# The last tokens in runs of 384 and 128 in place of 256 and 256, for the last down-projection and the final norm

## The chip, the cores and the metric

The kernel runs on one core of one Trainium2 chip, as one program. The metric is device time in microseconds (us) from launch to end, the median of several runs. A core has five engines that each work through a queue of their own: PE (TensorE, matrix products; its weight loads are listed apart as PEld), DVE (VectorE), ACT (ScalarE), POOL (GpSimd) and SP (SyncE, which here only issues transfers). They wait for each other through semaphores.

## The reference

A diffusion backbone of two layers works on 512 latent tokens (and, in the first layer, on 256 context tokens) of 1024 features. Each layer has a mixer (convolution, attention, gated linear attention) and a SwiGLU feed-forward of 2816 hidden features. The change concerns only the end of the second layer and what follows it, where the context tokens are no longer carried:

```python
x = x + gt2 * swiglu(rmsnorm(x, g2) * (1 + sc2) + sh2, w_up, w_down)   # last layer
return rmsnorm(x, final_norm_g)

def swiglu(h, w_up, w_down):
    a, b = jnp.split(h @ w_up, 2, axis=-1)
    return (jax.nn.silu(a) * b) @ w_down
def rmsnorm(x, g):
    return x * rsqrt(mean(x * x, -1) + 1e-6) * g
```

All inputs and the output (1, 512, 1024) are float32.

## The kernel before

**Layout.** The stream is held with features on the partitions: `xT[k]`, k from 0 to 7, is a tile of 128 features by 512 tokens. A run of tokens ("segment") is a triple (first, end, kind). `XS` is all 512 tokens; `XA` and `XB` are tokens 0 to 256 and 256 to 512. In the last layer `ga, gb = XA, XB`.

**Products.** For accuracy each float32 operand is split in two rounded parts (type float32r), hi and lo, and a product of matrices is three products on PE: hi by hi, hi by lo, lo by hi. ACT writes the hi part of a weight (a copy with rounding), DVE the lo part (a subtraction). `dense_pass(ws, X, segs, evict)` does one output block of 128 features for each segment: for every chunk of 128 input features three `S.mm`, each with weights of 128x128 and with as many columns as the segment has tokens, into a bank of PSUM of the kind "main" (three banks) and then `evict`. There are five banks of the kind "bank". All products are issued at line 139, all transposes at line 143; those are the lines of the helpers that the profile shows. Plain float32 products (not split) occur too, among them the sums over features with a column of ones.

**The hidden layer in blocks.** The 22 chunks of the hidden layer of the last layer come in blocks of 6, 6, 6 and 4 (`F_BLOCKS`). After each block its share of the down-projection is added to `xT` by `residual` (a DVE operation at line 199: PSUM times gate plus `xT`). The last block has 4 chunks. Its down-projection also has to deliver the squares for the final norm: `Sums.add` takes the square of the finished `xT[k]` on ACT (line 155) and adds it up on DVE (line 188), for each segment on its own.

**The tail.** `tail` does this last down-projection in an order of its own. Output blocks 0 and 1 were opened ahead (class `Opened`: their first three chunks fill PE while the last hidden chunk is being made), blocks 0, 1 and 2 are then done for both segments; blocks 3 to 7 are done for the first segment, their weights kept, the first segment's norm is handed on, and then blocks 3 to 7 are done for the second segment:

```python
for m in range(n_first, NK):                       # n_first = N_DOWN = 3
    ws.append((m, *w_next(keys[m]), 0))
    dense_pass(ws[-1:], X, (ga,), ev_)
norm_next(ga, sums[ga])
for j, w in enumerate(ws):
    dense_pass([w], X, (gb,), ev_)
    S.gave(plan[first + j]["b"])
S.gave(*drop)
norm_next(gb, sums[gb])
```

**The final norm.** `final_task(seg, sums)` is spawned for each segment. It becomes due `LAG_F` = 2100 ns (of the planner's time) after its spawning. It sums the squares over the partitions (one product with `ones` for each 128 tokens), takes the reciprocal root (`rstd`: DVE and ACT on a few columns), scales the eight `xT[k]` by the norm's weights in place (line 193: even k on DVE, odd k on POOL), and then for each 128 tokens transposes eight blocks back to tokens by features into two banks (line 143), scales them by the root (one half on DVE, line 193, one on ACT, line 181) and stores 512 KB from SP (line 2054).

**What sets the order.** The class `Plan` keeps a clock for each engine while the program is being written: an operation is booked at a cost (`COST`; for a rounded product `max(columns, 64) / 2.4` ns), and results are booked 150 ns (`HOP`) later. Tasks such as `final_task` are generators; `poll`, called after every chunk, steps those that are due by the planner's PE clock and for which there is room in the pools (`ROOM`: three main banks, five others). A bank counts as taken until the planned end of the operation that empties it. So the planner's costs decide between which products a task's instructions are put. Below it, the framework's scheduler may still move ready instructions of an engine ahead of others.

Of the kernel before, what the change touches and what calls it, by code (L numbers as in the profile page):

```python
# [20 lines left out]
SX = 512  # L21
# [21 lines left out]
CS = (SX, T, 1)  # L43
XA = (0, SX // 2, 0)
XB = (SX // 2, SX, 0)


C_ID, C_TL, C_TR, C_LV, C_BD, C_COS, C_SIN = 0, 128, 256, 384, 768, 896, 1408
# [271 lines left out]
def hybrid_kernel(ctx: ExitStack, tc: tile.TileContext, x, c, cx, c_ctx, w_mod, b_mod, norm1_g, norm2_g,  # L320
# [3 lines left out]
    S = Plan(tc)  # L324
# [16 lines left out]
    def tmp(rows=P, dt=F32):  # L341
        return S.took("t3", t3.tile([rows, T], dt, tag="t3", name="t3"))
# [83 lines left out]
    N_OUT2, N_DOWN = 1, 3  # L426
# [33 lines left out]
    for l in range(DEPTH):  # L460
# [19 lines left out]
        blocks = F_BLOCKS[l]  # L480
# [105 lines left out]
    def w_next(key):  # L586
        it = plan[at["use"]]
        assert it["key"] == key, (it["key"], key)
        if at["use"] and not plan[at["use"] - 1]["quarters"]:
            plan[at["use"] - 1]["read"] = True  # L590
        w_advance()
        at["use"] += 1
        if it["mod"]:
            S.last = max(S.last, it["t"])
        if it["quarters"]:
            return it
        return it["raw"] if it["mod"] else it["w"]
# [148 lines left out]
    def mod_steps():  # L746
        while at["use"] < len(plan) and plan[at["use"]]["mod"]:
            mod_step()
# [5 lines left out]
    def dense_pass(ws, X, segs, evict):  # L754

        n = len(X)
        for s in segs:
            t0, t1, _ = s
            S.room(main=len(ws))
            pts = [bank("main") for w in ws]  # L760
            for k in range(n):
                for (name, hi, lo, c0), pt in zip(ws, pts):
                    mm_ = 96 if name == "lr" else P
                    for a, b, st, sp in ((hi, 0, k == 0, False), (hi, 1, False, False), (lo, 0, False, k == n - 1)):
                        S.mm(pt[:mm_, :t1 - t0], a[:, k, c0:c0 + mm_], X[k][b][:, t0:t1], st, sp)
                S.poll()
            for w, pt in zip(ws, pts):
                evict(w[0], s, pt)
                S.gave(pt)
        S.poll()  # L770
# [497 lines left out]
    def split2(full, h, sl):  # L1268
        S.acopy(h[:, 0, sl], full)
        S.tt(h[:, 1, sl], full, h[:, 0, sl].bitcast(F32), ALU.subtract)  # L1270

    def residual(l, which, pt, m, s, sums=None):
        t0, t1, i = s
        S.stt(xT[m][:, t0:t1], pt[:, :t1 - t0], mod(l, which, m, i), xT[m][:, t0:t1], ALU.mult, ALU.add)
        if sums:
            sums[s].add(m)
# [454 lines left out]
    for l in range(DEPTH):  # L1731
        last = l == DEPTH - 1
        both = (XS, CS)
        sg = (XS,) if last else both
        ga, gb = (XA, XB) if last else (XS, CS)
        n = SX if last else T
# [191 lines left out]
        def tail(keys, X, which, n_first, norm_next, segs, drop, opened=()):  # L1928

            ga, gb = segs  # L1930
            sums = {s: Sums(s) for s in segs}
            ev_ = lambda m, s, pt: residual(l, which, pt, m, s, sums)
            for m in range(n_first):
                if m < len(opened):
                    opened[m].close(ev_)
                else:
                    dense_pass([(m, *w_next(keys[m]), 0)], X, segs, ev_)
                mod_steps()
            ws = []
            first = at["use"]  # L1940
            for m in range(n_first, NK):
# [8 lines that stand above are left out]
# [7 lines left out]
        blocks = F_BLOCKS[l]  # L1957
        units, made, opened = [], 0, []
        for bi, (f0, f1) in enumerate(blocks):
            ts_, tiles_ = [], []  # L1960

            def swiglu(sil, tt_):
                def ev_ab(name, s, pt):
                    t0, t1, _ = s
                    if name == "a":
                        S.act(sil[:, t0:t1], pt[:, :t1 - t0], AF.Silu)
                    else:
                        S.tt(sil[:, t0:t1], pt[:, :t1 - t0], sil[:, t0:t1], ALU.mult)
                        split2(sil[:, t0:t1], tt_, slice(t0, t1))
                tiles_.append(tt_)  # L1970
                ts_.append((tt_[:, 0], tt_[:, 1]))
                return ev_ab

            def begin(fs):

                units[:] = [Unit(l, f, norm) for f in fs]
                units[0].make("a11")
                units[0].make("s1")

            if bi == 0:  # L1980
                S.room(t3=2, act=2)
                sils = [tmp() for _ in range(2)]
                evs = [swiglu(sil, act_t(F32R)) for sil in sils]

                diff = []

                def hook0():
                    diff.append(S.spawn(norm.differences(("t1", "t2", "t3")), prio=-1,
                                        when=lambda: S.clk["pe"] if norm.done.get(gb, 0) == NK else None))
                Firsts((l, "up"), (ga, gb)).run(norm, lambda i, s, pt: evs[i % 2]("ab"[i // 2], s, pt),  # L1990
                                                (hook0, lambda: begin(range(2, f1))))
                S.gave(*sils)
                S.spawn(norm.differences(("t4",)), prio=-1, when=lambda: diff[0]["ready"] if diff[0]["done"] else None)
            heads = []

            def then():
                mod_steps()
                heads.append(w_next((l, "d", bi, 0)))
            run_units(units, 2, then)
            for u in units:  # L2000
                ts_.append(u.out)
                tiles_ += u.tiles

            ss = (ga, gb) if bi == len(blocks) - 1 else sg
            opened = [Opened((0, *heads[0], 0), ts_, ss)]
            opened.append(Opened((1, *w_next((l, "d", bi, 1)), 0), ts_, ss))
            if bi < len(blocks) - 1:
                ev_d = lambda m, s, pt: residual(l, 5, pt, m, s)
                for m in range(NK):
                    if m < len(opened):  # L2010
                        opened[m].close(ev_d)
                    else:
                        w = (m, *w_next((l, "d", bi, m)), 0)
                        if m == NK - 1:
                            begin(range(*blocks[bi + 1]))
                        dense_pass([w], ts_, sg, ev_d)
                    if m:
                        mod_steps()
                S.gave(*tiles_)
# [4 lines left out]
        keys = [(l, "d", len(blocks) - 1, m) for m in range(NK)]  # L2024
        if not last:
            norm = Normed(l + 1, V_N1, 1, 0)
            tail(keys, ts_, 5, N_DOWN, lambda s, sums: S.spawn(norm.task(s, sums), prio=-2), (ga, gb),
                 tiles_, opened)
        else:

            fin = []

            def final_task(seg, sums):
                t0, t1, _ = seg
                S.last += LAG_F
                yield dict(bank=1)
                pt = bank()
                nt = (t1 - t0) // P
                r = rstd(sums.total(pt), nt)
                S.gave(pt)  # L2040
                for k in range(NK):
                    S.ts(xT[k][:, t0:t1], xT[k][:, t0:t1], vec[:, V_FN + k:V_FN + k + 1], None, ALU.mult,
                         eng="pool" if k % 2 else "dve")
                for t in range(nt):
                    yield dict(bank=2)
                    pts = [bank(), bank()]
                    for k in range(NK):
                        S.tr(pts[k // 4][:, (k % 4) * P:(k % 4 + 1) * P], xT[k][:, t0 + t * P:t0 + (t + 1) * P], ident)
                    o = wp.tile([P, 1024], F32, tag="raw", name="raw", bufs=RAWS)
                    S.ts(o[:, :512], pts[0], r[:, t:t + 1], None, ALU.mult)  # L2050
                    S.amul(o[:, 512:], pts[1], r[:, t:t + 1])
                    S.gave(pts[0])
                    S.gave(pts[1])
                    nc.sync.dma_start(out[0, t0 + t * P:t0 + (t + 1) * P, :], o)
            tail(keys, ts_, 5, N_DOWN, lambda s, sums: fin.append(S.spawn(final_task(s, sums), prio=-2)), (ga, gb),
                 tiles_, opened)
            S.wait(*fin)

# [25 lines left out]
```

## Time and profile before

| what | us |
|---|---|
| median of the runs shown (three: 1618.64, 1619.19, 1624.01) | 1619.19 |
| the profiled execution, its own time | 1613.43 |
| its span, first to last instruction | 1611.6 |
| PE busy | 1569.9 (97% of the span) |
| DVE busy | 1219.3 (76%) |
| ACT busy | 757.0 (47%) |
| mean granted clock of PE | 0.997 of full speed |

The profiled execution is taken by the hardware profiler; times of instructions are counted from the span's start. A row of a group gives line, engine, operation, what it writes and reads by the program's names, shape and count, then busy time and mean duration of one. Products of a stream overlap, so their spacing is less than their duration. The chain of waits is followed back from the last instruction. The windows give busy time by engine for stretches of the span, with the count of instructions in brackets and the granted clock.

### The profile page before, as it was taken

How to read it: one execution, taken by the hardware profiler on the slowest of the kernel's cores; microseconds unless marked ns; L12 is line 12 of the kernel's file. 1: busy time of each engine (PE TensorE's matmuls, PEld its weight loads, DVE VectorE, ACT ScalarE, POOL GpSimd, SP SyncE). 2: the span in 40 equal slices, each digit the busy share in tenths (PEclk: the TensorE clock that was granted, in tenths of full speed). 3: DMA queues.
4: the chain of work that ended last, by engine and by line, in shares of the span. 5: the costliest groups of instructions: out<-in, count | busy, mean ns of one | idle time of the engine just before them, and what ended most of it. 6: DMA issues, size and time to landing. Idle time of an engine off the chain costs nothing.

```text
span 1611.6 us, 29142 instructions
## 1 busy us (share of the span) xinstructions
PE 1569.9 (97%) x11530; PEld 1387.9 (86%) x11530; DVE 1219.3 (76%) x2426; ACT 757.0 (47%) x1596; POOL 105.2 (7%) x122
## 2 busy tenths in 40 slices
PE   7999999999999999999999999998999999999998
PEld 5778777888888899999999988786889989989898
DVE  5687886668886788788888877879787956747576
ACT  4455544453663243242433546464474744536354
POOL 2000000000000000000000010000001112213012
PEclk9999999999999999999999999999999999999999
DMA  9831222253224544435334342211225466858552
GB/s 256 247 113 28 82 64 71 62 170 109 75 79 146 156 132 144 143 118 156 93 108 127 91 133 66 53 40 41 66 85 120 94 148 139 173 126 160 147 123 93
DMA packets 277578, 184.39 MB, mean 114 GB/s; under 512 B 30853, under 2 KB 258753, under 8 KB 277441
## 3 DMA queue, kind: packets, MB, share of 16 engines
q1 hardware_dynamic: 251008, 155.93, 33.7%
q0 software_dynamic: 24608, 21.27, 7.7%
q10 hardware_dynamic: 1824, 5.31, 0.9%
q8 instruction: 91, 1.49, 0.4%
q14 instruction: 47, 0.38, 0.1%
HBM read 175.14 MB, written 7.34 MB: 113 GB/s over the span
## 4 chain that ended last, share of the span: by engine, by line
PE 75%; DVE 10%; DMA 3%; ACT 3%; issue 2%; DVEq 0%; SPq 0%; ACTq 0%
PE main L139 49%; PE bank L139 24%; DVE act L188 3%; PE bank L143 3%; DMA raw<-in_w_mod_dram 2%; DVE t L188 1%; DVE wlo L188 1%; DMA raw<-in_w_up_dram 1%; ACT t L155 1%; DVE t L216 1%; DVE t L199 1%; DVE mx L207 1%; ACT t L177 1%; DVE t L193 0%; ACT whi L177 0%
## 5 line engine op out<-in xcount | busy, mean ns | idle before, releaser
L139 PE MATMUL main<-act,whi 128*128 128x512 f32 (+2 forms) x2772 | 667.8, 345 | 5.6 <-DVE act L199 2.1
L139 PEld LDWEIGHTS main<-act,whi 128*128 128x128 f32 x2772 | 460.5, 189 | 63.6 <-issue 12.1
L139 PE MATMUL main<-act,wlo 128*128 128x512 f32 (+2 forms) x1866 | 477.7, 334 | 3.0 <-DVE wlo L188 3.0
L139 PEld LDWEIGHTS main<-act,wlo 128*128 128x128 f32 x1866 | 315.1, 189 | 31.7 <-DVE wlo L188 5.2
L177 ACT CAST whi<-raw 128x512 fp32r<-128x512 f32 (+4 forms) x242 | 181.5, 751 | 292.6 <-PE main L139 201.0
L139 PE MATMUL bank<-act,whi 128*128 128x256 f32 (+2 forms) x1140 | 208.9, 309 | 1.1 <-DVE whi L188 0.7
L139 PEld LDWEIGHTS bank<-act,whi 128*128 128x128 f32 x1140 | 178.5, 190 | 8.1 <-DVE whi L188 1.0
L139 PE MATMUL bank<-act,wlo 128*128 128x256 f32 (+2 forms) x898 | 171.7, 308 | 2.2 <-DVE wlo L188 2.2
L199 DVE SCALAR_TENSOR_TENSOR act<-main,mods,act 128x256 f32<-128x256 f32 (+1 forms) x162 | 99.1, 615 | 78.1 <-PE main L139 76.6
L139 PEld LDWEIGHTS bank<-act,wlo 128*128 128x128 f32 x898 | 142.8, 190 | 6.3 <-DVE wlo L188 3.2
L188 DVE TENSOR_TENSOR wlo<-raw,whi 128x1024 fp32r<-128x1024 f32 (+4 forms) x122 | 122.6, 1005 | 20.7 <-ACT whi L177 19.9
L188 DVE TENSOR_TENSOR wlo<-raw,wlo 128x512 fp32r<-128x512 f32 x120 | 81.6, 686 | 39.4 <-ACT wlo L177 38.7
L199 DVE SCALAR_TENSOR_TENSOR t<-raw,cst,t 128x512 f32<-128x512 f32 x126 | 92.1, 745 | 20.4 <-DMA raw<-in_w_mod_dram 19.8
L188 DVE TENSOR_TENSOR whi<-raw,whi 128x512 fp32r<-128x512 f32 x120 | 81.3, 686 | 26.2 <-ACT whi L177 24.6
L155 ACT ACTIVATE t<-bank,nm 128x256 f32<-128x256 f32 (+1 forms) x144 | 69.8, 497 | 60.4 <-DVE nm L199 55.7
L177 ACT CAST wlo<-raw 128x512 fp32r<-128x512 f32 x120 | 74.6, 622 | 40.9 <-PE main L139 17.4
L177 ACT COPY t<-bank 128x512 f32<-128x512 f32 (+3 forms) x131 | 57.4, 453 | 72.1 <-PE bank L139 43.5
L139 PE MATMUL main<-act 128*128 128x256 f32 (+1 forms) x516 | 79.5, 309 | 0.0
L188 DVE TENSOR_TENSOR act<-t,act 128x512 fp32r<-128x512 f32 (+7 forms) x110 | 73.1, 681 | 7.0 <-ACT act L177 5.2
L155 ACT ACTIVATE t<-t 128x256 f32<-128x256 f32 (+3 forms) x108 | 58.1, 538 | 41.8 <-DVE t L188 41.3
L139 PE MATMUL main<-t,whi 128*128 128x512 f32 (+1 forms) x302 | 75.9, 338 | 0.0
L139 PEld LDWEIGHTS main<-act 128*128 128x128 f32 x516 | 70.9, 191 | 5.2 <-ACT t L155 0.4
(162 smaller groups left out, 2007.3 us busy)
## 6 DMA issues: line engine op xcount, KB each, us to landing
raw<-in_w_mod_dram SPq DMA_DIRECT2D x92, 512.0 KB, 4.3
raw<-in_w_up_dram SPq DMA_DIRECT2D x80, 512.0 KB, 4.6
raw<-in_w_in_dram SPq DMA_DIRECT2D x26, 512.0 KB, 3.9
t<-in_w_up_dram POOLq DMA_DIRECT2D x40, 256.0 KB, 5.2
raw<-in_w_down_dram SPq DMA_DIRECT2D x24, 384.0 KB, 3.9
raw<-in_w_down_dram SPq DMA_DIRECT2D x32, 256.0 KB, 2.8
raw<-in_w_down_dram SPq DMA_DIRECT2D x16, 320.0 KB, 3.4
raw<-in_w_up_dram POOLq DMA_DIRECT2D x20, 256.0 KB, 4.7
```

The lines of the kernel that those rows point to most:

```text
L139: self.pin("pe", self.nc.tensor.matmul(out, lhsT, rhs, start=start, stop=stop, **kw))
L143: self.pin("pe", self.nc.tensor.transpose(out, in_, ident))
L155: ins = self.pin("act", self.nc.scalar.activation(out, in_, func, **kw))
L177: self.pin("act", self.nc.scalar.copy(out, in_))
L188: self.pin(eng, self._v(eng).tensor_tensor(out, a, b, op))
L199: self.pin(eng, self._v(eng).scalar_tensor_tensor(out, a, s, b, op0, op1))
L207: self.pin("dve", self.nc.vector.tensor_reduce(out, in_, AX.X, op))
L216: self.pin("dve", self.nc.vector.copy_predicated(out, mask, data))
```

## The change

For the last block of the last layer the two segments are tokens 0 to 384 and 384 to 512. This goes for the openings of blocks 0 and 1, for the whole of `tail` there and so for the sums of squares and for both `final_task`s (three tiles of 128 tokens in the first, one in the second). The rest of the last layer, its other tail after the mixer included, keeps 256 and 256.

```diff
+XE, XF = (0, 384, 0), (384, SX, 0)
...
-            ss = (ga, gb) if bi == len(blocks) - 1 else sg
+            ends = (XE, XF) if last else (ga, gb)
+            ss = ends if bi == len(blocks) - 1 else sg
             opened = [Opened((0, *heads[0], 0), ts_, ss)]
             opened.append(Opened((1, *w_next((l, "d", bi, 1)), 0), ts_, ss))
...
-            tail(keys, ts_, 5, N_DOWN, lambda s, sums: fin.append(S.spawn(final_task(s, sums), prio=-2)), (ga, gb),
+            tail(keys, ts_, 5, N_DOWN, lambda s, sums: fin.append(S.spawn(final_task(s, sums), prio=-2)), ends,
                  tiles_, opened)
```

## The prediction

> **What bounds the kernel now.** I read the page first, then the chain of waits for the last 40 us, then the windows over the last stage, and last the timeline of PE for the price of one product of each width.
>
> ```profile
> span 1611.6 us, 29142 instructions
> PE 1569.9 (97%) x11530; PEld 1387.9 (86%) x11530; DVE 1219.3 (76%) x2426; ACT 757.0 (47%) x1596; POOL 105.2 (7%) x122
> PE 75%; DVE 10%; DMA 3%; ACT 3%; issue 2%; DVEq 0%; SPq 0%; ACTq 0%
> ```
>
> PE is busy for 97% of the span, so work added to it is paid in full unless it falls where PE waits. The change touches only the end, so that end is what has to be read (chain of waits, start, length, what):
>
> ```profile
> 1582.63 13.14 PE main L139 x108
> 1595.77 0.34 PE bank L139 x4
> 1596.11 2.98 PE main L139 x24
> 1599.09 0.87 PE bank L143 x8
> 1599.96 1.45 PE main L139 x12
> 1601.42 0.03 issue
> 1601.44 0.48 DVE act L199
> 1601.93 0.70 DVE raw L193
> 1602.63 0.34 DVE t L188
> 1602.97 0.14 issue
> 1603.11 0.59 PE bank L139 x4
> ...
> 1605.25 0.75 DVE raw L193
> 1606.00 0.66 DVEq L2080
> ```
>
> ```profile
> core 0: us, PE busy (x) PEld busy (x) DVE busy (x) ACT busy (x) POOL busy (x), PEclk, DMA share, GB/s
> 1576.30:1582.35 6.05, 6.05 (x51) 5.87 (x49) 3.68 (x7) 3.71 (x6) 0.00 (x0) 1.00 0.45 129
> 1582.35:1592.90 10.55, 10.55 (x89) 10.43 (x88) 10.09 (x26) 5.45 (x14) 5.45 (x4) 1.00 0.10 27
> 1592.90:1601.40 8.50, 8.50 (x74) 8.50 (x74) 6.26 (x20) 3.01 (x8) 3.47 (x3) 1.00 0.00 1
> 1601.40:1611.60 10.20, 3.26 (x29) 2.81 (x26) 3.74 (x10) 2.71 (x6) 1.20 (x1) 0.87 0.53 207
> ```
>
> Two regimes follow. Up to 1601.4 us, here called T, PE has no gap and its granted clock is 1.00: the last down-projection is bound by PE alone, and DVE (10.09 of 10.55 us in the first run's passes) is just covered. From T to the end there are 10.2 us of latency: residual, square, sum, root, scaling, store. The change makes the first regime dearer or not, and the second shorter or not.
>
> **The price of one product.** Before, every product of the stage has 256 columns. After, half have 384 and half 128. From rows of the timeline (start, length, xcount; the spacing is the length less the last one's own duration, over count less one):
>
> ```profile
> 1563.23 3.04 PE L139 MATMUL main<-act,whi 128*128 128x256 f32 x24
> ...
> 465.60 2.24 PE L139 MATMUL bank<-act,whi 128*128 128x384 f32 x12
> ...
> 1598.93 1.03 PE L143 MATMUL bank<-tab,act 128*128 128x128 f32 x8
> ...
> 1603.11 0.58 PE L139 MATMUL bank<-ones,t 128*128 128x1 f32 x4 [0.83 <-DVE t L188]
> ...
> 141.29 1.28 PE L139 MATMUL bank<-t,t 128*128 128x128 f32 x10
> ```
>
> ```profile
> L139 PE MATMUL main<-act,whi 128*128 128x256 f32 x1080 | 182.5, 286 | 1.4 <-ACT act L155 1.2 <-DVE act L199 0.2
> ...
> L139 PE MATMUL bank<-act,whi 128*128 128x384 f32 x360 | 68.0, 335 | 1.1 <-DVE whi L188 0.7 <-ACT whi L177 0.5
> ...
> L139 PE MATMUL bank<-t,t 128*128 128x128 f32 x80 | 10.4, 277 | 0.0
> ...
> L139 PE MATMUL bank<-ones,t 128*128 128x1 f32 x40 | 5.0, 235 | 0.8 <-DVE t L188 0.8
> ```
>
> ```profile
> L139 PEld LDWEIGHTS main<-act,whi 128*128 128x128 f32 x2772 | 460.5, 189 | 63.6 <-issue 12.1 <-ACT whi L177 3.9 <-ACT act L155 2.2
> ...
> L139 PEld LDWEIGHTS bank<-t,t 128*128 128x128 f32 x80 | 9.8, 191 | 0.6 <-issue 0.2 <-ACT t L177 0.2
> ```
>
> 256 columns: (3.04 - 0.29)/23 = 0.120 us. 384 columns: (2.24 - 0.335)/11 = 0.173 us. So 128 further columns cost 0.053 us, and by that line 128 columns alone would cost 0.067. Then 384 + 128 would equal 256 + 256 and the change would be free on PE. The short rows say that it is not: a product of a single column (ones) still takes (0.58 - 0.24)/3 = 0.11, eight transposes of 128 columns (1.03 - 0.27)/7 = 0.109, and ten plain float32 products of 128 columns (1.28 - 0.28)/9 = 0.112. Every product brings its own weight load, and the load of a rounded operand is as long as that of a plain one (189 and 191 ns), so I put the floor at 0.11.
>
> No row has a rounded (float32r) product of under 256 columns: all of them in this kernel are 256, 384 or 512 wide, and this is the unknown of the case. Bounds: 0.067 below (the line of streaming alone), and above, what a plain float32 product of 128 columns costs. The program asks for five such products at 141.29 and ten records stand there, so it is two records each: 2 x 0.112 = 0.223, should the narrow form lose the single pass. I take 0.112, since the rows nearest in width, one record each, all lie at 0.109 to 0.112; I keep both ends.
>
> The Trainium skill (TensorE: Matmul & The Clock Gate, section Back-to-back issue gap) gives a sustained 81 ns for load and product of 128 columns. By it the PE sum below would be 96 x (0.173 + 0.081) - 23.04 = +1.3 us in place of +4.3; the rows of this trace at 0.109 to 0.112 for four-byte weights do not agree.
>
> **The change part by part.**
>
> 1. *Passes.* Eight output blocks, four chunks of the last block of the hidden layer, three products each (hi by hi, hi by lo, lo by hi): 96 products in each run of tokens. Before 96 x 2 x 0.120 = 23.04 us; after 96 x (0.173 + 0.112) = 27.36. That is +4.32 us, all of it ahead of T, where PE has no gap. With 0.223 it is 38.02, +14.98.
>
> 2. *The order of the final norm.* Program order comes from a planner that books a product of 128 columns at 128/2.4 = 53 ns, so a second-run pass at 640 ns in place of 1,280, and makes the first run's final task due 2,250 ns after that run's last product. Before, this fell in the second of the five second-run passes, and the trace has the sum there (1595.77, four records). Then, by the planner's own costs, the task books eight scalings one after another, and its first tile falls due 7,504 ns after the run's end; three main banks were held by evictions booked behind them, the fifth pass had to wait, and so the first tile's eight transposes went ahead of it (1599.09, 0.87 us, in the chain). After: the sum falls in the fourth pass, only that pass's bank is held behind the scalings, the fifth pass finds a free one, and the first tile falls due near 8,300 ns, long after the passes (booked to end near 3,560). So 0.87 us leave the path ahead of T. The first run's sum has three products in place of two, two records each by the row of four above: +0.22 us. Net of 1 and 2: T moves by 4.32 - 0.87 + 0.22 = +3.67 us.
>
> 3. *The end after T.* What gets shorter: residual, square and sum over 128 in place of 256 columns. They lie in the chain with 0.48, 0.42 (ACT's row below) and 0.34 us; bounds 0 and half of it, 0 to 0.6 us saved, and I take the middle, 0.3. The sum loses one product of two records, 0.22. What gets longer: before, one tile was done ahead of T (its transposes at 1599.09), one in the shadow of the wait for the sum, two at the very end. After, four tiles are left: 32 transposes at 0.109 (3.5 us), and four scalings on DVE and ACT side by side:
>
> ```profile
> 1605.25 1.41 DVE L193 TENSOR_SCALAR raw<-bank,rst 128x512 f32<-128x512 f32 x2
> ...
> 1601.96 0.42 ACT L155 ACTIVATE t<-act 128x256 f32<-128x256 f32 x1 [1.27 <-DVE act L199]
> ...
> 1605.24 1.27 ACT L181 ACTIVATE raw<-bank,rst 128x512 f32<-128x512 f32 x2 [0.88 <-DVE rst L188]
> ...
> 1600.72 6.35 SPq L2054 DMA_DIRECT2D out_dram<-raw  x4
> ...
> DMA to landing us min/median/max: 2.6/2.9/3.3
> ...
> 1602.47 1.20 POOL L193 TENSOR_SCALAR act<-act,vec 128x256 f32<-128x256 f32 x1 [2.59 <-ACT t L155]
> ```
>
> One scaling takes 0.75 and 0.69 us. Before, the last ends at 1605.25 + 1.41 = T + 5.3. After, there are five banks: one for the sum, two for a tile, two for the next; so tiles go at most two at a time, and each pair of transposes and scaling takes 0.87 + 0.75. If the first run's tiles start right at T, the four scalings end near T + 5.2; if PE takes the second sum first and waits for it, near T + 6.4. The stores are queued by SP behind these scalings, 512 KB each, the last issued at 1607.07 - 0.33 = 1606.74 and landed 3.3 later, at 1610.0; a last store by itself lands in 2.6. So the end moves by -0.1 - 0.5 = -0.6 to +1.1 us against T; I take +0.4. POOL's scaling of the last block (1.20 us, after the square) gets shorter and ends well ahead of the transposes.
>
> 4. *Costing nothing.* The first run's residual, square and sum over 384 columns and DVE's scalings: DVE has 10.09 of 10.55 us booked in that window, but the window itself grows by 5 x 12 x 0.053 = 3.2 us; without this cover the weight splits of the held blocks would be late. POOL has 5.45 of 10.55 there. Transfers are at 27 GB/s and less: no load is waited for.
>
> Sum: +3.67 + 0.4 = +4.1 us. The profiled execution took 1613.43 us (span 1611.6 and 1.8 around it), 5.8 below the median of the runs, 1619.19; the difference is added to the median: 1623.3 us, +0.25%. About 0.3% (4.9 us) is what can be told from no change.
>
> **The rivals.**
>
> *The narrow product loses its single pass* (slower). Place: the second run's 96 products, and the point that decides is whether 128 columns of the rounded type take one record at 0.11 or cost what plain float32 does. At 0.223: +14.98 - 0.65 + 0.4 = +14.7 us, 1633.9. For it: rounded products stand only at 256 columns and more, and plain float32 takes two records of 0.112 each at the very width 128. Against it: nothing in the trace shows a width at which a form changes; 256, 384 and 512 lie on one line. The Trainium skill (FP8 and Floating Point Precision, section TensorE Precision Notes) says that true float32 takes four passes; the two records at 0.112, twice the streaming of 128 columns each, agree, but no run here shows the narrow rounded form.
>
> *Load and product overlap better than in the transposes, and the short end wins* (not slower). At 0.067 PE's share is nil: -0.65 + (-0.6 to 0.4) = -1.3 to -0.2 us, 1618 to 1619; it decides from a spacing of about 0.07 down. Against it: the one-column row at 0.11. The 81 ns of the Trainium skill (the same section of TensorE: Matmul & The Clock Gate as above) lie in this case, and by them the time would be 1.3 - 0.65 + 0.4 = +1.1 us, 1620.2.
>
> *DVE becomes the bound in the first run's passes.* It has 0.46 us to spare now and gains 3.2; each pass adds at most half of the residual's 0.48 and the sum's 0.34, 0.41 us, 2.1 in five. No cost by this, but if a split came late it would show as PE waiting for act, up to 1 us.
>
> **How the numbers follow.** Single pass at about 0.112: 0.53; two records' worth: 0.40; well under 0.11: 0.07. The likeliest gives 1623.3, its own range with a spacing up to 0.120 (+0.8) and the end from -0.6 to +1.1: 1622 to 1625.5. Slower by over 0.3%: all of the second and about a third of the first, 0.58; within 0.3%: 0.39; faster 0.03. The range leaves out the third case and reaches to the second: 1620.5 to 1635.
>
> **What would show it.** Spacing of the products 128x128 out of whi and wlo in the last stage: 0.11 or 0.22. 384-wide at 0.173. Transposes of the first run's tiles all behind the last pass. T near 1605 (or near 1616), and about 10.5 us from T to the end. Wrong would make it a PE gap ahead of T, or transposes between the passes.

## The result, and the profile after

| | before | after |
|---|---|---|
| median of six runs each, side by side, us | 1618.48 (1616.26 to 1624.01) | 1630.95 (1628.0 to 1635.0) |
| ratio, with its 95% interval | | 1.0071 (1.0056 to 1.0086) |
| the profiled execution, its own time, us | 1613.43 | 1629.65 |

The change costs 11.5 us by the ratio (9.1 to 13.9), where +4.1 was forecast. The sign and the rows that price a product were right, and two terms were far too small. One execution in twelve of kernel e8 below, at a granted clock of 0.557, took 2530 us, and its ratio leaves that one out.

The span of the kernel after; lines of this kernel and of most experiments have numbers two higher than before:

```profile
span 1627.7 us, 29134 instructions
```

The spans differ by 16.1 us. To see what of it the change can own, I cut both at the last table load of ACT, which stands just ahead of the openings of blocks 0 and 1, and at T, the end of the last product of the down-projection. The windows of before, then of after (stretch and its length, busy time with count for PE, PEld, DVE, ACT, POOL, then granted clock, DMA share, GB/s):

```profile
1576.07:1601.40 25.33, 25.33 (x211) 25.02 (x210) 20.03 (x51) 12.40 (x27) 8.92 (x7) 1.00 0.15 42
1601.40:1611.65 10.25, 3.26 (x29) 2.81 (x26) 3.74 (x10) 2.71 (x6) 1.20 (x1) 0.87 0.52 206
```

```profile
1582.06:1614.10 32.04, 29.17 (x203) 28.38 (x201) 20.43 (x48) 12.40 (x26) 8.44 (x7) 1.00 0.11 34
1614.10:1616.00 1.90, 0.40 (x2) 0.40 (x3) 1.04 (x4) 0.31 (x1) 0.68 (x1) 0.67 0.00 0
1616.00:1621.40 5.40, 5.40 (x26) 5.40 (x27) 2.95 (x8) 1.78 (x4) 0.02 (x1) 0.50 0.26 106
1621.40:1627.74 6.34, 1.02 (x9) 0.78 (x7) 0.75 (x1) 1.38 (x2) 0.00 (x0) 0.77 0.60 240
```

The table load begins 6.0 us later after (1582.06 against 1576.07). Ahead of it ACT has the same instructions in the same order in both kernels, and the median of before lies 5.05 above its profiled execution, that of after only 1.3: those 6.0 us I put down to the two executions, not to the change. In the kernels of the experiments it begins anywhere from 1575.39 to 1581.35, and not by kernel: 1576.48 in e8, which has the change, 1581.27 in e9, which doesn't. From the table load to the end it is 35.58 us before and 45.68 after: +10.1, inside the interval of the ratio. This splits in two. Up to T it takes 6.7 us more, of which PE works 3.84 (29.17 less 25.33) and idles 2.87; before, it had no gap there. From T to the end it takes 13.64 in place of 10.24, +3.4, and for the 5.40 us of the third window, all within that, the granted clock is at half.

**The gap ahead of T.** The timeline of PE in after (start, length, operation, count, and in brackets the idle time before it and what ended that):

```profile
1591.43 0.62 PE L141 MATMUL main<-act,whi 128*128 128x384 f32 x2 [1.90 <-ACT whi L179]
1593.02 0.45 PE L141 MATMUL main<-act,wlo 128*128 128x384 f32 x1 [0.97 <-DVE wlo L190]
1593.30 0.51 PE L141 MATMUL main<-act,whi 128*128 128x384 f32 x2
...
1593.83 0.51 PE L141 MATMUL main<-act,whi 128*128 128x384 f32 x2
...
1595.15 0.39 PE L141 MATMUL main<-act,whi 128*128 128x128 f32 x2
...
1595.48 0.39 PE L141 MATMUL main<-act,whi 128*128 128x128 f32 x2
```

PE has closed blocks 0 and 1 and waits for the weights of block 2, hi from ACT (1.90) and then lo from DVE (0.97). The same rows give the price of a product: three products of 384 columns from 1593.30 to 1593.83 are 0.177 each (0.174 over longer stretches), three of 128 from 1595.15 to 1595.48 are 0.11, one record each. Why the weights come late is seen on ACT. Its timeline, before and then after, and DVE's after:

```profile
1578.41 1.14 ACT L177 CAST act<-raw 128x512 fp32r<-128x512 f32 x2
1581.87 0.62 ACT L177 CAST whi<-raw 128x512 fp32r<-128x512 f32 x1 [2.33 <-issue]
...
1583.03 1.13 ACT L177 CAST act<-raw 128x512 fp32r<-128x512 f32 x2
...
1584.68 0.61 ACT L177 CAST act<-raw 128x512 fp32r<-128x512 f32 x1
```

```profile
1584.40 1.14 ACT L179 CAST act<-raw 128x512 fp32r<-128x512 f32 x2
1588.45 0.62 ACT L179 CAST act<-raw 128x512 fp32r<-128x512 f32 x1 [2.91 <-DMA raw<-in_w_down_dram]
1589.28 0.62 ACT L179 CAST act<-raw 128x512 fp32r<-128x512 f32 x1 [0.21 <-DMA raw<-in_w_down_dram]
1590.24 0.62 ACT L179 CAST act<-raw 128x512 fp32r<-128x512 f32 x1 [0.34 <-DMA raw<-in_w_down_dram]
1590.77 0.61 ACT L179 CAST whi<-raw 128x512 fp32r<-128x512 f32 x1
```

```profile
1590.89 0.69 DVE L190 TENSOR_TENSOR act<-raw,act 128x512 fp32r<-128x512 f32 x1 [0.27 <-ACT act L179]
1591.50 0.61 DVE L201 SCALAR_TENSOR_TENSOR act<-main,mods,act 128x384 f32<-128x384 f32 x1
...
1592.29 0.68 DVE L190 TENSOR_TENSOR wlo<-raw,whi 128x512 fp32r<-128x512 f32 x1
```

The cast into `whi` is block 2's; the casts into `act` are of weights kept for the second run, blocks 3 to 7. Before, block 2's came third, ahead of blocks 5 to 7. After, it is the last of the six: ACT's queue stands in it behind three casts that each wait for a transfer of weights PE needs only later. DVE's queue stands the same way: its subtraction for block 2 (1592.29) comes behind the one for block 7 (1590.89), which had to wait for that block's cast, and behind residuals (line 201).

**The end.** PE's timeline of after, from the last passes on:

```profile
1611.89 2.20 PE L141 MATMUL main<-act 128*128 128x128 f32 x18
1615.60 0.59 PE L141 MATMUL bank<-ones,t 128*128 128x1 f32 x2 [1.50 <-DVE t L190]
1616.05 6.37 PE L145 MATMUL bank<-tab,act 128*128 128x128 f32 x32
```

All 32 transposes stand behind the second run's sum, for whose squares PE waits 1.50 us. Then they run at about 0.21 each (26 in 5.40 us, with the window's clock at 0.50), where the prediction's row of eight gives 0.109.

### The profile page after: what moved, and what is told of

It reads as the page before. It is cut to its first block, busy times and chain, and to the rows that moved or that the text cites. A ratio compares the mean times of both kernels' runs of the same rounds, so it can differ in the third digit from the quotient of the medians.

```text
span 1627.7 us, 29134 instructions
## 1 busy us (share of the span) xinstructions
PE 1578.6 (97%) x11524; PEld 1397.2 (86%) x11530; DVE 1221.3 (75%) x2426; ACT 757.5 (47%) x1596; POOL 104.3 (6%) x122
## 4 chain that ended last, share of the span: by engine, by line
PE 74%; DVE 10%; DMA 4%; ACT 3%; issue 2%; DVEq 0%; ACTq 0%
PE main L141 47%; PE bank L141 24%; PE bank L145 3%; DVE act L190 3%; DMA raw<-in_w_mod_dram 2%; DVE wlo L190 1%; DVE t L190 1%; DMA raw<-in_w_up_dram 1%; ACT t L157 1%; DVE t L201 1%; DVE t L218 1%; DVE act L201 1%; ACT act L157 1%; DVE mx L209 1%; ACT t L179 1%
## 5 line engine op out<-in xcount | busy, mean ns | idle before, releaser
L141 PE MATMUL main<-act,whi 128*128 128x512 f32 (+3 forms) x2780 | 671.2, 346 | 7.5 <-ACT whi L179 2.9
L141 PE MATMUL bank<-act,whi 128*128 128x256 f32 (+3 forms) x1132 | 208.6, 310 | 4.9 <-DVE whi L190 4.1
L201 DVE SCALAR_TENSOR_TENSOR act<-main,mods,act 128x512 f32<-128x512 f32 (+3 forms) x163 | 99.5, 615 | 76.8 <-PE main L141 75.0
L141 PE MATMUL main<-act 128*128 128x256 f32 (+3 forms) x516 | 81.8, 313 | 0.0
L190 DVE TENSOR_TENSOR t<-t,t 128x256 f32<-128x256 f32 (+5 forms) x106 | 63.6, 607 | 17.7 <-ACT t L157 16.6
```

The costliest lines, as they stand in the source:

```text
L141: self.pin("pe", self.nc.tensor.matmul(out, lhsT, rhs, start=start, stop=stop, **kw))
L190: self.pin(eng, self._v(eng).tensor_tensor(out, a, b, op))
L201: self.pin(eng, self._v(eng).scalar_tensor_tensor(out, a, s, b, op0, op1))
```

## The experiments

Each was read like this. "Stretch" runs from the last table load to the end in the profiled execution; the ratio is that of the timed runs to the kernel before beside them.

| kernel | table load to T | T to the end | stretch | ratio to before (95%) |
|---|---|---|---|---|
| before | 25.33 | 10.24 | 35.58 | |
| after | 32.03 | 13.64 | 45.68 | 1.0071 (1.0056 to 1.0086) |
| e1_d2_first | 29.07 | 12.58 | 41.65 | 1.0037 (1.0023 to 1.0052) |
| e2_book_256 | 32.80 | 9.20 | 42.00 | 1.0047 (1.0031 to 1.0064) |
| e3_both | 29.92 | 9.19 | 39.12 | 1.0022 (1.0007 to 1.0036) |
| e4_warm | 31.89 | 11.78 | 43.67 | 1.0054 (1.0035 to 1.0072) |
| e5_before_tiles_late | 24.44 | 13.12 | 37.55 | 1.0002 (0.9985 to 1.0018) |
| e7_tiles_fill_wait | 24.44 | 11.55 | 36.00 | 0.9992 (0.9976 to 1.0008) |
| e8_wide_head | 27.78 | 9.19 | 36.97 | 0.9997 (0.9980 to 1.0014) |
| e9_wide_head_before | 24.04 | 10.33 | 34.37 | 0.9985 (0.9968 to 1.0003) |

In every row the change of the stretch against before lies inside the interval of the ratio (taken times 1616 us): +6.1 against 3.7 to 8.4 for e1, +3.5 against 1.1 to 5.8 for e3, and so on. The ratio of one kernel can't tell a difference of a microsecond. The stretch is of one execution each; where two kernels share a part, it repeats closely (up to T 31.89 in e4 and 32.03 in after, the end 9.19 to 9.20 in e2, e3 and e8), but e7 and e9, with the same order at the end, differ there by 1.2 us.

**e1_d2_first: the order on ACT and DVE alone.** The kernel after, with block 2's cast and split placed ahead of block 5's on their engines:

```diff
-                S.acopy(hi, it["raw"])
-                S.tt(lo, it["raw"], hi.bitcast(F32), ALU.subtract)
+                c_ = S.acopy(hi, it["raw"])
+                s_ = S.tt(lo, it["raw"], hi.bitcast(F32), ALU.subtract)
+                if it["key"] == (1, "d", 3, 2):
+                    at["d2"] = c_, s_
+                if it["key"] == (1, "d", 3, 5):
+                    S.behind(c_, at["d2"][0])
+                    S.behind(s_, at["d2"][1])
```

> Changed kernel, with the rounding of block 2's weights (whi, and its lo part) ordered ahead of block 5's on ACT and DVE; nothing else moves. Theory A (the wait in the changed kernel is made by the order on ACT: block 2's cast stands behind three casts that wait for late transfers): PE's gap of 1.90 + 0.97 us after the close of blocks 0 and 1 falls to about 0.4, the stretch from the first opened product to the end goes from 45.3 to about 42.8 us, and the time to about 1.0055 of before. Rival (PE waits there for the transfer itself or for a free weight buffer, whatever the order): the gap stays above 2 us and the stretch at 45.

Measured: median 1623.06, ratio 1.0037. ACT's timeline, the window up to T, and PE's timeline after T:

```profile
1587.92 0.62 ACT L179 CAST whi<-raw 128x512 fp32r<-128x512 f32 x1 [3.09 <-issue]
```

```profile
1581.35:1610.42 29.07, 28.96 (x203) 28.32 (x201) 20.05 (x48) 11.98 (x26) 8.42 (x7) 1.00 0.13 37
```

```profile
1611.93 0.38 PE L141 MATMUL bank<-ones,t 128*128 128x1 f32 x2 [1.51 <-DVE t L190]
1612.18 5.36 PE L145 MATMUL bank<-tab,act 128*128 128x128 f32 x32
```

PE's idle time ahead of T falls from 2.87 to 0.11 us, and table load to T by 2.96. The order of block 2's weights in the two queues was the whole gap; the edit moves the cast and the subtraction together, so ACT's share is not shown apart from DVE's. The end is 1.06 us shorter too, which was not expected: PE waits for the second sum as in after, but the transposes behind it take 5.36 us in place of 6.37. What made the framework's scheduler choose the order of after was not tried. That block 2's buffer is released later, since the opened blocks hold PE for longer, is my reading of the code; the traces fit it, but do not prove it: counted from the table load, block 2's cast starts at 5.80 us before and at 6.57 in e1, and in after block 5's, which went ahead, at 6.39.

**e2_book_256: the planner's price alone.** The kernel after, with a rounded product booked as at least 256 columns:

```diff
-        c = max(n, 64) * (4 if rhs.dtype == F32 else 1) / 2.4
+        c = max(n, 256 if rhs.dtype == F32R else 64) * (4 if rhs.dtype == F32 else 1) / 2.4
```

> Changed kernel, with the planner booking a rounded product of 128 columns like one of 256, which puts the first run's sum after the second of the second run's passes, one tile's eight transposes ahead of the last pass and eight more behind it, ahead of the second sum. Theory B (the end is long because all 32 transposes come behind a wait of PE of 1.5 us and run at half the granted clock): the spacing of the last transposes goes from 0.213 back to about 0.11, the end after the last product from 13.6 to about 10.5 us, T itself 0.9 later, net -2.2 us. Rival (the four stores of 512 KB at the end set its length): end above 12.5 us, net about zero.

Measured: median 1625.24, ratio 1.0047. The windows:

```profile
1579.19:1611.99 32.80, 30.04 (x213) 29.39 (x212) 21.60 (x51) 12.97 (x27) 8.42 (x7) 1.00 0.11 33
1611.99:1621.20 9.21, 3.06 (x26) 2.61 (x25) 3.50 (x10) 2.88 (x7) 0.60 (x1) 0.86 0.57 228
```

The end falls from 13.64 to 9.20. PE works 0.87 more ahead of T, which is a tile's eight transposes back in front of it, and the gap (32.80 less 30.04) stays at 2.76. Booked at the higher price, the first run's first tile comes ahead of the last six products and its second behind them, into PE's wait for the second sum, and the end is then 1.04 us shorter than before's.

**e3_both: e1 and e2 together.** What is left is the widths themselves.

> Changed kernel with both edits: block 2's weights first, and products of 128 columns booked like 256. If A and B and the arithmetic of the products (96 x (0.173 + 0.111 - 0.240) = 4.3 us, and 0.2 for a longer first sum) make up the whole, the stretch from the first opened product to the end is 35.2 + 5.0 = 40.2 to 40.6 us and the time about 1.003 to 1.0035 of before. If something else is at work: above 42.

Measured: median 1620.15, ratio 1.0022. The windows, PE's timeline at the end, the scaling behind the second sum's root, and the stores:

```profile
1579.37:1609.29 29.92, 29.81 (x213) 29.30 (x212) 21.19 (x51) 12.57 (x27) 8.42 (x7) 1.00 0.12 36
1609.29:1618.49 9.20, 3.06 (x27) 2.61 (x25) 3.50 (x10) 2.89 (x7) 0.60 (x1) 0.90 0.57 228
```

```profile
1607.61 1.06 PE L145 MATMUL bank<-tab,act 128*128 128x128 f32 x8
1608.43 0.87 PE L141 MATMUL main<-act 128*128 128x128 f32 x6
1609.13 1.06 PE L145 MATMUL bank<-tab,act 128*128 128x128 f32 x8
1610.89 0.35 PE L141 MATMUL bank<-ones,t 128*128 128x1 f32 x2 [0.70 <-DVE t L190]
1611.10 1.95 PE L145 MATMUL bank<-tab,act 128*128 128x128 f32 x16
...
1613.28 0.75 DVE L195 TENSOR_SCALAR raw<-bank,rst 128x512 f32<-128x512 f32 x1
...
DMA to landing us min/median/max: 2.6/2.7/2.7
```

Table load to T is 4.59 us longer than before. With one tile ahead of T in both, the prediction's rows give 4.32 + 0.22 = 4.54 for it. The end is 1.05 shorter, which the expectation had not counted, so the whole is +3.5 us where +5.0 was expected. This is not because the second sum comes sooner: it starts 1.60 us behind T (1610.89) against 1.71 before, and the scaling behind its root starts at T + 3.99 against T + 3.85. But one tile stands behind that root in place of two: its scaling ends at T + 4.74 against T + 5.26, and its store lands within 2.7 us where the last of before took 3.3. So 384 and 128 do buy a shorter end, but pay 4.59 us for 1.05. The two cures add up but for 1.15 us: after less e1 is 4.03 us of stretch, after less e2 3.68, after less e3 6.56. Of the 1.15, 1.06 is the shorter end of e1, which e2 takes away as well.

**e4_warm: the half clock alone.** The kernel after, with seven products of zeros into a bank that nothing reads, put into PE's wait for the second sum:

```diff
+            if gb == XF:
+                S.room(bank=1)
+                pt = bank()
+                for _ in range(7):
+                    S.mm(pt, zero[:, :P], zero, True, True)
+                S.gave(pt)
             norm_next(gb, sums[gb])
```

> Changed kernel with seven products of zeros (512 columns, 1.5 us) put between the last pass and the second sum, where PE waits; the order of everything else is kept. Theory B with the clock as the cause: PE has no gap there, the granted clock stays at 1, the 32 transposes come at 0.11 in place of 0.213, and the end after the last real product goes from 13.6 to about 11 us. Rival (the transposes are slow because each tile waits for banks or for the scalings): spacing by tile stays at 1.7 us and the end within 0.5 us of 13.6.

Measured: median 1626.07, ratio 1.0054. PE's timeline, the window from T, and the transfers from 1614.5 to 1623.1 in 40 slices (GB/s):

```profile
1611.06 1.69 PE L141 MATMUL bank<-zero 128*128 128x512 bf16 x7
...
1612.97 3.69 PE L145 MATMUL bank<-tab,act 128*128 128x128 f32 x32
```

```profile
1611.22:1623.00 11.78, 5.45 (x42) 4.19 (x39) 4.56 (x13) 3.47 (x8) 0.70 (x1) 0.83 0.45 179
```

```profile
GB/s 0 0 0 0 0 286 419 419 381 419 400 400 419 419 362 457 381 381 457 343 419 438 362 400 476 362 400 457 343 153 0 0 0 0 0 0 0 0 0 0
```

With the wait filled, the 32 transposes take 3.69 us in place of 6.37, spaced by 0.11, and the end falls by 1.86, to 11.78. It does not fall by the 2.68 that PE saves. The transfers say why: four stores issued close together keep the queues at some 400 GB/s for 5.4 us without a pause, so the stores become the limit of the end. In these profiles, then, 1.86 of the end's 3.4 us are the clock and 1.54 the rest. The order alone costs more than that: e2 has the same widths with the tiles in the better order, and its end of 9.20 is 2.58 shorter than e4's; the 1.04 that one tile less behind the last root saves has to be taken off. Whether every execution of after loses the clock is not shown; the last section comes back to it.

**e5_before_tiles_late: the order alone, at 256 and 256.** The kernel before, with all tiles held back until the second run's sum is done:

```diff
+            def held():
+                return any(done)
...
+                done.append(t0 > 0)
...
-                    yield dict(bank=2)
+                    yield dict(bank=lambda: 2 if held() else 99)
```

> Kernel before, runs of 256 and 256 kept, with one part of the change's effect alone: the first run's two tiles (transposes, scalings, stores) wait until the second sum has been issued, as the planner did it in the changed kernel. Theory B (the order of the tiles and the half clock behind PE's wait): the last product ends 0.9 us earlier, PE then waits about 1.5 us, transposes come at 0.21 for a while, the end after the last product goes from 10.2 to 12.5-13.6 us, and the stretch from the last table load on ACT to the end from 35.6 to 37-38.5 us; about 1.001 of before. Rival (it is the runs of 384 and 128 that make the end long): the end stays under 11 us.

Measured: median 1617.23, ratio 1.0002. PE's timeline, and the stores:

```profile
1605.14 0.61 PE L139 MATMUL bank<-ones,t 128*128 128x1 f32 x4 [1.61 <-DVE t L188]
1605.61 3.69 PE L143 MATMUL bank<-tab,act 128*128 128x128 f32 x32
```

```profile
DMA to landing us min/median/max: 3.9/4.3/4.7
```

T comes 0.89 earlier, the eight transposes that left the path, and the end is 2.88 longer; in the ratio this can't be told from no change. The half clock that I had expected here did not come: the wait of PE is as long as in after (1.61 against 1.50), yet the transposes run at 0.11. The longer end comes from the order and from the stores, which land 3.9 to 4.7 us after their issue where those of before took 2.6 to 3.3. So at these widths the order costs up to 2.88 at the end, near the 2.58 between e4 and e2. Not all of it need be the order: in e4 four stores issued as closely land in 2.7 to 3.9 us, and what made all four slower here is not shown. A wait of this length alone does not make the clock drop.

**e7_tiles_fill_wait and e9_wide_head_before: the better order for the kernel before.** e7 holds the tiles until the second run's norm is handed on, so that two tiles fill PE's wait for the second sum; the edit is that of e5 with another condition:

```diff
+            def held():
+                return len(fin) == 2
```

> Kernel before, runs of 256 and 256, with the first run's first tile moved from ahead of the last pass to behind it, so that both tiles' 16 transposes fill PE's wait for the second sum. Theory: the last product ends 0.87 us earlier, the clock stays up, the end after it is 10.2 to 10.6 us; stretch from the last table load to the end 34.7 to 35.1 in place of 35.6, about 0.9995 of before, less than the runs can tell. Rival (the scaling of the moved tile on DVE holds up the second run's sum): end 11 us, nothing gained.

Measured: median 1615.1, ratio 0.9992. The window from T, and the transfers from 1601 to 1611.4 in 40 slices:

```profile
1599.84:1611.39 11.55, 4.12 (x36) 3.68 (x34) 4.52 (x12) 3.35 (x7) 1.24 (x1) 0.78 0.47 183
```

```profile
GB/s 0 0 0 0 0 268 441 394 347 441 426 394 378 362 410 95 32 441 410 378 425 425 394 394 394 410 347 32 32 16 32 16 0 0 0 0 0 0 0 0
...
DMA to landing us min/median/max: 4.5/4.5/4.5
```

T comes 0.88 earlier as forecast and PE's wait is gone. The end is 1.3 longer than before's, where at most 0.4 longer was expected. The rival isn't the reason: the second sum starts 1.78 us behind T, against 1.71 before. The stores are: each takes 4.5 us to land, and for the last 1.3 us of the transfers only 16 to 32 GB/s flow where some 400 did. What makes them late is not shown. e9 has the same order and shows the end without it. Its other edit is that of e8.

**e8_wide_head: the price of a product, tested by taking products out.** e3, with blocks 0 to 2, which are done for both runs anyway, as one product of 512 columns in place of 384 and 128; the eviction still goes by runs:

```diff
+            def ev_all(m, s, pt):
+                for g in segs:
+                    residual(l, which, pt[:, g[0]:g[1]], m, g, sums)
...
-                    opened[m].close(ev_)
+                    opened[m].close(ev_all if whole else ev_)
...
-                    dense_pass([(m, *w_next(keys[m]), 0)], X, segs, ev_)
+                    dense_pass([(m, *w_next(keys[m]), 0)], X, (XS,) if whole else segs, ev_all if whole else ev_)
...
-            ss = ends if bi == len(blocks) - 1 else sg
+            ss = ((XS,) if last else ends) if bi == len(blocks) - 1 else sg
```

> The kernel of e3_both (384 and 128, block 2's weights first, products booked like 256) with the first three output blocks, which are done for both runs anyway, computed in one product of 512 columns and emptied in parts of 384 and 128. If what is left of the loss is the price of the products (0.173 + 0.111 = 0.284 against 0.240 for 256 + 256), then 36 pairs at 0.227 in place of 0.284 give back 2.05 us: from the last table load to the last product 29.9 to 27.9 us, stretch 39.1 to 37.1, ratio to before about 1.001. Rival (PE is no longer the bound there, DVE's weight splits or the evictions are): less than 1 us comes back and gaps appear on PE.

Measured: median 1615.55, ratio 0.9997. The window up to T:

```profile
1576.48:1604.26 27.78, 27.78 (x177) 25.60 (x176) 20.99 (x51) 12.68 (x27) 9.05 (x7) 1.00 0.13 39
```

36 products fewer (213 to 177 in the first window) shorten table load to T by 2.14 us, 0.06 each; 0.174 + 0.11 less the 0.23 at which the 512-wide ones are spaced in the timeline gives 0.054. So the price of the split products is confirmed, and PE has no gap there, which the rival needed. With this the widths 384 and 128 can't be told from before, though the stretch is still 1.4 us longer.

For e9, that edit on e7, at 256 and 256:

> The kernel of e7_tiles_fill_wait (256 and 256) with the first three output blocks computed in one product of 512 columns and emptied in halves. 36 x (0.240 - 0.227) = 0.47 us less on PE; stretch from the last table load to the end 34.2 to 34.6 us. Rival (evictions in one lump delay the next pass): PE shows gaps and the stretch is above 35.

Measured: median 1615.1, ratio 0.9985. The window from T and the stores:

```profile
1605.31:1615.64 10.33, 4.13 (x36) 3.68 (x34) 4.52 (x12) 3.35 (x7) 1.24 (x1) 0.90 0.51 203
```

```profile
DMA to landing us min/median/max: 2.6/2.9/3.3
```

The stores, issued at the same distance from T as in e7, land in 2.6 to 3.3 here, and the end is 10.33. The stretch is 1.2 us shorter than before's, within what was expected. The interval of the ratio still reaches 1, so this is the best version tried and not shown to beat the kernel before.

## Why the prediction was right in sign and short in size

The measured 1630.95 lies inside the stated range of 1620.5 to 1635, but by luck. The range reached that far for a narrow product of two records, which did not come. The likeliest case had a range of its own, up to 1625.5 (its own terms, 3.67 + 0.8 + 1.1 on 1619.19, give 1624.8), and the measured time lies above it.

**What bounds the kernel.** PE without a gap up to T was the right picture of before. It was carried over to after without asking whether PE's inputs would still come in the old order.

**Step 1, the passes (+4.32).** Right. 128 columns cost 0.11 in one record, and e3, with both disturbances taken out, shows 4.59 for passes and longer sum against 4.54. The rival of two records (0.223, +14.7) falls: its time, 1633.9, is nearer to the measured 1630.95 than the forecast is, but no row supports its mechanism; the products of 128 columns in the last passes have 60 records for five times twelve products. So does the overlap at 0.067 or at the sustained 81 ns of the Trainium skill (TensorE: Matmul & The Clock Gate, section Back-to-back issue gap), with which this trace, at 0.11, does not agree.

**Step 2, the order of the final norm (-0.87 and +0.22).** Right. The transposes all came behind the last pass, and the planner's price is the reason, as said: e2 changes that price alone, and a tile goes back ahead of the last six products. The finer path that the step gives, which bank is held and which pass finds one free, was not tested.

**Step 3, the end after T (+0.4).** Wrong in size: +3.4. The step left open whether PE would take the first tiles or the second sum first, had -0.6 and +1.1 for the two, and took a value between. PE took the sum. With the clock kept up (e4) the end is +1.54, 0.44 above that bound, which fits four stores running into each other. It is made up of 2.58 for the order (e4 less e2) and -1.04 for one tile less behind the last root (e2 less before). The other 1.86 is the half clock, on which the step had no term: the prediction's window after T already had a mean of 0.87, and I did not ask when in it the clock falls (at about 1609, behind PE's last product). Right in it was that the shorter second run saves at the end, 1.05 us in e2 and e3 where the step had 0.3 + 0.22; but the traces put that on one tile less behind the root, not on the shorter residual, square and sum that the step named.

**Step 4, costing nothing.** This is the step that failed outright. "No load is waited for" was read off GB/s, which says that the transfers have room, not that every one has landed when its reader's turn comes. In after ACT waits for three loads, with block 2's cast behind them, and PE waits 1.90 us for that cast and 0.97 for DVE's subtraction behind it: 2.87 us. The rival on DVE's splits had named the right sign in the trace, PE waiting for weights; its "up to 1 us" fits the 0.97, but not the larger wait for ACT, on which no term stood. The cover by ACT was never costed, because ACT is busy for less than half of the time.

The sum with these sizes: 3.67 up to T as forecast, + 2.87 for the gap, + 3.4 at the end = 9.9, against 10.1 in the profiles and 11.5 (9.1 to 13.9) in the runs. Of the two signs of being wrong, the gap of PE ahead of T came; transposes between the passes did not.

## What to carry to other kernels

Splitting a run of columns unevenly isn't free when one part falls to a width at which the spacing has stopped shrinking, here 0.11 us at 128 columns as at one: price both widths by rows, as 384 at 0.174 and 128 at 0.11 against twice 0.120. When a change alters how long an engine holds its buffers or what a planner books, ask for every cast or copy on a lightly loaded engine what now stands ahead of it in that queue and what that waits for; busy shares and GB/s don't show it. A new wait of PE just ahead of a row of products may cost half the clock behind it: fill it with work that is there anyway (e2's and e7's tiles) before filling it with dummies. When an uneven split puts less work behind the last wait, count what stands behind it, here one tile and one store in place of two.

## What the runs showed that was not expected

- In after a PE wait of 1.50 us was followed by 5.40 us at a granted clock of 0.50, and the clock came back while nothing but transposes ran. In e1 the same wait (1.51) left 32 transposes at 5.36 us in place of 3.69, and in e5 a wait of 1.61 changed nothing. Windows of half a microsecond put the fall in after at about 1614.7, inside the wait, and the return at 1621.6; in e1 the fall comes at 1612.9, 1.0 us behind the wait's end, and the return at 1616.3: 6.8 and 3.4 us at half. That a wait alone does not decide it shows in code that no edit touches. Before and e7 are the same program there, and PE waits as long ahead of the same 32 products; yet before keeps its clock, and e7 is at half for 6.8 us. PE's timeline, before and then e7, and the windows in the same order:

```profile
1120.13 0.69 PE L139 MATMUL bank<-act,t 64*64 64x64 f32 x32 [1.40 <-ACT t L177]
...
1119.55 1.13 PE L139 MATMUL bank<-act,t 64*64 64x64 f32 x32 [1.39 <-ACT t L177]
```

```profile
1118.00:1122.00 4.00, 2.04 (x40) 1.12 (x40) 4.00 (x11) 3.96 (x12) 0.00 (x0) 1.00 0.36 96
1118.00:1122.00 4.00, 2.60 (x38) 1.60 (x38) 4.00 (x12) 3.37 (x10) 0.00 (x0) 0.52 0.46 131
```

So the 1.86 us are what one execution of after lost, and that e4 kept its clock is one execution too. The Trainium skill (TensorE: Matmul & The Clock Gate, section Why this matters for your kernels) advises against gaps of PE of over some 3 us; here half that was enough in two executions of three. The same page (section What's actually happening) has the clock follow activity in a window that runs freely, at about 3.4 us; the 3.4 and 6.8 us at half agree with it, and a fall that depends on where the wait lies in such a window would fit, but no run here varies the place of one wait alone, and it stays open.

- Stores of 512 KB issued closer than about 1.3 us queue up behind each other at some 400 GB/s (e4, e5), so at the end of e4 a faster engine could have brought nothing: its stores follow each other without a pause.
- Late stores cost about 1.2 us at the end of one profile (e7, 4.5 us to landing) and not of another with the same issues (e9, 2.6 to 3.3).
